# A hybrid convolution and delta-rule block on one core: convolutions without zero margins, large tiles of 4,096 bytes from an address that is a multiple of 256, and a new order of the first half

## The chip, the core and the metric

The kernel runs on one core of a Trainium2 chip, in one launch. The metric is device time in microseconds, the median of three runs. The core has five engines with a queue each: TensorE (PE, matrix products into eight PSUM banks), VectorE (DVE), ScalarE (ACT), GpSimd (POOL) and SyncE (SP). In this kernel SP issues all transfers between the on-chip SBUF and HBM. "PEld" in the profile is TensorE's weight load, which runs beside its products.

## What is computed

One layer on 1,024 positions with 1,024 channels, all in float32. The part that the change touches, from the reference:

```python
h = rms_norm(x, g_mix[i])
proj = h @ w_in[i]
glu_a, glu_b, q, k, v, z, a_in, b_in, gate_a, gate_b = split_cols(proj, IN_SIZES)

c = glu_a * jax.nn.sigmoid(glu_b)
c = depthwise_conv(c, conv_dw_w[i]) + conv_dw_b[i]
c = jax.nn.silu(layer_norm(c, conv_ln_g[i], conv_ln_b[i]))
y_conv = c @ w_conv_out[i]

qkv = jax.nn.silu(depthwise_conv(jnp.concatenate([q, k, v], axis=-1), qkv_conv_w[i]))
```

The first convolution is 31 positions wide, the second 5. Both are centred and run per channel over the positions, with zeros outside. Behind them come the gated delta rule on q, k and v (eight heads, forward and backward), an output product for each branch, a merge by two gates, a product with `w_o`, a gated feed-forward part of width 2,816 and a per-layer embedding with a gate.

## The kernel before

**Layout and products.** Channels lie on the 128 partitions and positions along the free dimension, so a block is 128 channels by 1,024 positions, worked on in two halves of 512. A float32 operand of a large product is split into two parts of type float32r, high and low (`split`, line 709: ScalarE makes the high part, VectorE the rest), and each product is three matmuls (`mm3`, line 760): high by high, high by low, low by high. The stationary operand is mostly a weight tile w (128 x 128 of it at a time), the moving one 512 columns of a large tile. Matmuls of 128 columns in plain float32 serve the delta rule and the transposes.

**Two halves.** The first half is the input projection (eight blocks each of q, k, v, z, of the two halves of the GLU and of two gates), the two convolutions, the layer norm with the first output product, and the delta rule of the heads. The second half is the output product of the delta rule, the merge, `w_o`, the feed-forward part and the embedding.

**Who sets the order.** The program first records its operations (`Plan.add`, line 191), each with an engine, a cost and a level. `Plan.order` (line 347) then runs through them as through a simulation: on each engine it picks, of what is ready, the operation of the lowest level, and it hands out the slots of the tiles as they come free. The levels of the parts stand in `LV` (line 573), the number of tiles that a part may hold in `CAP` (line 574): `raw5` and `acc5` are the input and the result of the short convolution, `wmain` and `wfill` the weight tiles of the main stream and of the fill, `bank` the PSUM banks of small products. `MAIN` (line 607) and `FILL` (line 609) list the blocks of the projection in the order in which they are recorded: `k0` is block 0 of k, `g0` the GLU with its wide convolution, `a4` and `b5` blocks of the two gates, `l0` the decay and beta logits, `p0` the projection of the embedding. Every block of the projection loads its weights in two transfers of 256 KB (`load_w`, line 718), and most store their result.

**Where tiles lie.** SBUF is given out in this order: constants, 32 large slots (line 633), middle tiles of 2,048 bytes (19 of them: 8 + 4 + 4 + 3), small tiles (6,272 bytes), six weight tiles of 4,096 bytes (line 636). A large slot is as wide as the widest tile that ever lies in one. That is c of the wide convolution, [128, 1,024 + 30] floats (line 1027), 4,216 bytes, rounded up to 4,224. The constants end at byte 24,384, so large slots start at 64 and 192 modulo 256 in turn. Weight tiles start at 204,736 and every 4,096 from there, 192 modulo 256. Most high and low parts of a moving operand are the two halves of one slot (`half_pair`, line 776); those of the normed input hT, which the whole projection uses, lie in two slots (`act_pair`, line 773).

**The convolutions.** `do_qkv` (line 979) has ScalarE copy the product from PSUM into a tile with two zero columns at either end, which GpSimd fills, and `conv` (line 963) takes the first tap on ScalarE and four on VectorE, each over 1,024 columns shifted by one. `conv31` (line 997) works on even and odd positions apart: with u the sum of the even part of the input over the sums of neighbouring taps and v, going on from u, a sum over differences of odd and even parts, 31 taps take 46 steps of 512 columns where two separate sums would take 62. Its input c has zero margins that GpSimd fills in three places (lines 1032 to 1034).

Of the kernel before, what the change touches and what calls it, by code (L numbers as in the profile page):

```python
# [15 lines left out]
AF = mybir.ActivationFunctionType  # L16
ALU = mybir.AluOpType
# [527 lines left out]
P = 128  # L545
D = 1024
T = 1024
KB = D // P
NJ = T // P
NH = 8  # L550
CK = 31
SK = 5
# [3 lines left out]
HW = 512  # L556
# [6 lines left out]
def hs(h):  # L563
    return slice(h * HW, (h + 1) * HW)


def cs(j):
# [2 lines left out]


N_BIG, N_MID, N_W, N_D = 32, 8, 6, 11
LV = dict(w=-3.3, logits=-0.2, delta=-1.8, qkv=1.3, glu=1.5, z=-0.4, conv31=2.4, gate=2.3, pl=-0.3, ln=0.3, cout=2.55, ssq=-1.8)
CAP = dict(raw5=6, acc5=3, cpad=10, acc31=1, dif=1, lnev=3, wmain=4, wfill=2, bank=2, x0=4)
LEAD = (1, 3, 4)
PAIRS = (3, 3, 2, 2)
NS = sum(PAIRS)
# [26 lines left out]

MAIN = ("k0 v0 q0 l0 g0 z0 q1 z2 k1 g1 v1 g2 a4 z1 v2 q3 k2 k5 v3 b5 z3 q2 k3 k4 z4 q4 g3 v5 z6 v4 g4 q5 "
        "k7 q6 g6 g5 a7 z5 a5 v6 q7 a6 v7 k6 a0 g7 z7")
FILL = "a2 a3 b7 a1 b2 b0 b1 b3 p0 b4 b6"
PL_AFTER = 2  # L610


def ORDER(f):
# [3 lines left out]
          "a": lambda i: f["do_gate"](0, i), "b": lambda i: f["do_gate"](1, i)}  # L617
    for w in (MAIN + " " + FILL).split():
        do[w[0]](int(w[1:]))
# [5 lines left out]
def hybrid_block(tc, x, p, g_mix, w_in, conv_dw_w, conv_dw_b,  # L625
# [3 lines left out]
    pn = Plan(tc)  # L629
# [12 lines left out]
    def large(shape=None, dtype=F32, line="t", cap=99):  # L642
        return big.tile(shape or [P, T], dtype, tag="big", line=line, cap=cap)
# [9 lines left out]

    proj_cap, bank_cap = [2], [CAP["bank"]]

    def ev2():
        return medium()
# [8 lines left out]
    def const(name, shape):  # L666
        return cp.tile(shape, tag=name)
# [11 lines left out]
    for _ in range(WARM):  # L679
        ps = ps_.tile([P, HW], tag="ps", line="warm", cap=1)  # L680
# [7 lines left out]
    ident2 = const("ident2", [64, 32])  # L688
    pn.tt(ident2, ident[:64, 0:32], ident[:64, 32:64], ALU.add)

    half16 = const("half16", [P, 16])
    pn.fill(half16, 0.5)
    mhalf16 = const("mhalf16", [P, 16])
    pn.fill(mhalf16, -0.5)

    beta = const("beta", [P, 16, NJ])
# [7 lines left out]
    pl_s = const("pl_s", [P, 2, NJ])  # L704
    taps = const("taps", [P, KB, CK + 3 * SK])
    cw31s = const("cw31s", [P, KB, CK // 2 + 1])


    def split(hi, lo, src, scale=None):
# [8 lines left out]
    def load_w(w, r0, nk, c0, cap=4, pool=None):  # L718

        lv, parts = pn.level, []  # L720
        st = "main" if pn.stream == "main" else "rest"
        pn.level = LV["w"] if 1 <= lv < 3 else lv
        for k0 in range(0, nk, 4):
            n = min(4, nk - k0)
            raw = mid.tile([P, 4, P], tag="raw", bufs=4, line="raw", cap=2 if cap < N_W else 4, stream=st)
            if pool is None:
                t = wp.tile([P, 2, 4, P], F32R, tag="w", line="w", cap=cap, stream=st)
            else:
                t = pool([P, 2, 4, P], F32R, line="hp")
            rows_ = w[(r0 + k0) * P:(r0 + k0 + n) * P, c0:c0 + P]  # L730
            pn.dma(raw[:, :n], rows_.rearrange("(k q) c -> q k c", q=P))
            split(t[:, 0, :n], t[:, 1, :n], raw[:, :n])
            parts.append(t)
        pn.level = lv
        return parts
# [20 lines left out]
    def gated(out, t, v):  # L756

        pn.stt(out, t, 1.0, v, ALU.add, ALU.mult)
# [58 lines left out]
    x0 = [large(line="xt", cap=8) for _ in range(8)]  # L817
# [8 lines left out]
    col = {}  # L826
    def vectors(r, names):
        r0, vr = r, medium([64, P], line="vr")
        for name, v in names:
            n = v.shape[1] // P  # L830
            pn.dma(vr[r - r0:r - r0 + n, :], v[0].rearrange("(k q) -> k q", q=P))
            col[name] = vec_t[:, r:r + n]
            r += n
        ps = bank()
        pn.transpose(ps[:, :r - r0], vr[:r - r0], ident[:r - r0, :r - r0])
        pn.copy(vec_t[:, r0:r], ps[:, :r - r0])
        return r


    n = vectors(0, VEC[:1])  # L840
    pn.stream = "main"
    first = MAIN.split()[0]
    first_w = [load_w(w_in[0], 0, KB, C_Q + ("qkv".index(first[0]) * NH + int(first[1:])) * P)]
# [19 lines left out]
    def x_turned(h, k):  # L863
        ps = ps_.tile([P, HW], tag="ps", line="x0", cap=CAP["x0"])
        for i in range(4):
# [17 lines left out]
    NT = CK + 3 * SK  # L883
    raw = large([NT, D], line="taps")
# [4 lines left out]
    ps = bank()  # L889
# [6 lines left out]

    pn.tt(cw31s[:, :, :CK // 2], taps.at(0, [(NT, KB), (2, CK // 2)]), taps.at(1, [(NT, KB), (2, CK // 2)]), ALU.add)
    pn.copy(cw31s[:, :, CK // 2:], cw31[:, :, CK - 1:])


    to(0.4, "start")
# [7 lines left out]
    def logits():  # L909
        to(LV["logits"], "logits")  # L910
        wr = medium([P, KB, 32], line="wab")
# [47 lines left out]

    def load_cols(c0, cap=CAP["wmain"]):  # L960
        return load_w(w_in[0], 0, KB, c0, cap)

    def conv(acc, src, w, n, bias=None):
        pn.act(acc, src[:, 0:T], AF.Copy if bias is None else AF.Identity, scale=w[:, 0:1], bias=bias)
        for t in range(1, n):
            pn.stt(acc, src[:, t:t + T], w[:, t:t + 1], acc, ALU.mult, ALU.add)

    d_qkv = [[dp.tile([P, T], tag="dqkv%d_%d" % (i, j), bufs=1) for j in range(NH)] for i in range(3)]
    d_kk = [dp.tile([P, T], tag="dkk%d" % j, bufs=1) for j in range(NH)]
    d_y = [[spill() for _ in range(2)] for _ in range(KB)]  # L970
# [8 lines left out]
    def do_qkv(which, hd):  # L979
        to(LV["qkv"], "main", "qkv")  # L980
        b = which * NH + hd
        w = first_w.pop() if first_w else load_cols(C_Q + b * P)
        raw = large([P, T + SK - 1], line="raw5", cap=CAP["raw5"])
        for h in range(2):
            ps = block_half(w, hA, h, KB)
            pn.act(raw[:, 2 + h * HW:2 + (h + 1) * HW], ps)
        pn.fill(raw[:, 0:2], 0.0)
        pn.fill(raw[:, T + 2:T + 4], 0.0)
        acc = large(line="acc5", cap=CAP["acc5"])
        conv(acc, raw, taps[:, hd, CK + which * SK:CK + (which + 1) * SK], SK)  # L990
        pn.act(acc, acc, AF.Silu)
        pn.dma(d_qkv[which][hd], acc)

    lnacc = large(line="lnacc")
    CH = (T + CK - 1) // 2

    def conv31(c, b):

        w, ws = cw31[:, b], cw31s[:, b]
        co, ce = c[:, :CH], c[:, CH:2 * CH]
        dif = large([P, 2, CH], line="dif", cap=CAP["dif"])
        pn.tt(dif[:, 0], ce, co, ALU.subtract)
        pn.tt(dif[:, 1, :CH - 1], ce[:, 1:], co[:, :CH - 1], ALU.subtract)
        acc = large([P, 2, HW], line="acc31", cap=CAP["acc31"])
        u, v = acc[:, 0], acc[:, 1]
        pn.act(u, co[:, 0:HW], AF.Identity, scale=ws[:, 0:1], bias=col["cb31"][:, b:b + 1])
        n = CK // 2
        for t in range(1, n + 1):  # L1010
            pn.stt(u, co[:, t:t + HW], ws[:, t:t + 1], u, ALU.mult, ALU.add)
        for t in range(n + 1):
            pn.stt(c.at(0, [(2, HW)]) if t == n else v, dif[:, 0, t:t + HW], w[:, 2 * t:2 * t + 1],
                   v if t else u, ALU.mult, ALU.add)
        for t in range(n):
            pn.stt(c.at(1, [(2, HW)]) if t == n - 1 else u, dif[:, 1, t:t + HW], w[:, 2 * t + 1:2 * t + 2],
                   u, ALU.mult, ALU.add)

    def do_glu(b):
        to(LV["glu"], "main", "glu")  # L1020
        wb = load_cols(C_GLUB + b * P)
        sg = [ev2(), ev2()]
        for h in range(2):
            half_tanh(sg[h], block_half(wb, hA, h, KB))
        wa = load_cols(C_GLUA + b * P)

        c = large([P, T + CK - 1], line="cpad", cap=CAP["cpad"])
        for h in range(2):
            pa = block_half(wa, hA, h, KB)
            gated(c.at(7 + h * HW // 2, [(CH + 1, 2), (1, HW // 2)]), sg[h].at(0, [(1, 2), (2, HW // 2)]),  # L1030
                  pa.at(0, [(1, 2), (2, HW // 2)]))
        pn.fill(c[:, 0:7], 0.0)
        pn.fill(c[:, CH - 8:CH + 8], 0.0)
        pn.fill(c[:, 2 * CH - 7:2 * CH], 0.0)
        to(LV["conv31"], "conv31")
        conv31(c, b)
        acc = c[:, :T]
        for h in range(2):
            pn.dma(d_y[b][h], acc[:, hs(h)])
        if b == 0:  # L1040
            pn.copy(lnacc, acc)
        else:
            pn.tt(lnacc, lnacc, acc, ALU.add)

    def do_gate(i, b):
        to(LV["gate"], "fill", "gate")
        w = load_cols((C_GA, C_GB)[i] + b * P, CAP["wfill"])
# [468 lines left out]
    for k in range(HK):  # L1516
        raw = [large([P, 2, HW], line="o", cap=O_CAP) for _ in range(2)]
# [48 lines left out]
    for b in range(0, KB, 2):  # L1566
# [6 lines left out]
        s = medium(line="gs", cap=1)  # L1573
# [5 lines left out]
        g1 = mid.tile([P, HW], tag="m2", line="p1", bufs=4)  # L1579
# [56 lines left out]
    for h in range(2):  # L1636
        pn.sec = "wo"

        n = WO_LEAD if h == 0 else 0
# [15 lines left out]
        for k in range(HK):  # L1655
            for b in (k, k + HK):
                v = xT[b][:, hs(h)]
# [143 lines left out]
    ws = []  # L1801
# [132 lines left out]
    p0 = 0  # L1934
# [68 lines left out]
    for t in range(NJ - 1):  # L2003
# [3 lines left out]
        for c in range(2):  # L2007
            v = x3[t][:, hs(c)]
# [4 lines left out]
    t, n = NJ - 1, HW // 2  # L2013
    e = x3[t]
    v = [e[:, HW + i * n:HW + (i + 1) * n] for i in range(2)]
# [46 lines left out]
```

## Time and profile before

| | |
|---|---|
| median of three runs | 2059.19 us (2057.17 to 2059.95) |
| span of the profiled execution | 2056.1 us |
| TensorE busy | 2032.3 us (99%), 9,985 matmuls |
| VectorE busy | 1591.0 us (77%) |
| ScalarE busy | 1109.6 us (54%) |
| GpSimd busy | 123.8 us (6%) |
| transfers | 288.6 MB, 43.3% of the time of 16 DMA engines |

The span is that of one profiled execution, from its first to its last instruction; the runs are timed from outside, 3.1 us above it. "Busy" counts a matmul from its start to its modelled end, and the next one starts before that, so the time that a matmul takes in a stream is read from the distance of starts. Stretches of time are given in us from the span's start.

### The profile page before, as it was taken

To read this page: it belongs to the slowest core of one execution; us is meant where nothing else is said; L and a number is where in the kernel's file an instruction comes from. 1 tells how busy PE (TensorE), PEld (TensorE's weight loads), DVE (VectorE), ACT (ScalarE), POOL (GpSimd) and SP (SyncE) were. 2 spreads that over 40 slices of the span, in tenths; PEclk is the share of its full clock that TensorE was granted. 3 is DMA by queue.
4 is the path that set the end of the run, shared out by engine and by line. 5 is a ranking of instruction groups with operands and counts; after the bars stand their busy time and mean duration, and the time that the engine had idled before them with its cause. 6 is when DMAs were issued, how large, how long until landed. Compare 5 with 4: busy or idle time off the path is not lost.

```text
span 2056.1 us, 29043 instructions
## 1 busy us (share of the span) xinstructions
PE 2032.3 (99%) x9985; PEld 1670.9 (81%) x9985; DVE 1591.0 (77%) x2814; ACT 1109.6 (54%) x2627; POOL 123.8 (6%) x211
## 2 busy tenths in 40 slices
PE   8999999999999999999999999999999999999998
PEld 6888788888888888888888788887878877887887
DVE  5549999877959999997587876796666657889955
ACT  7635674566766675747865554433333335434462
POOL 1000111001100210011100000000000000000010
PEclk9999999999999999999999999999999999999999
DMA  5532432443333332534578676433323328534232
GB/s 195 167 97 98 140 108 89 149 136 103 112 127 127 108 95 85 200 113 165 175 256 277 199 251 190 144 114 106 103 89 116 102 82 292 169 110 130 86 107 103
DMA packets 278753, 288.60 MB, mean 140 GB/s; under 512 B 17767, under 2 KB 196128, under 8 KB 278606
## 3 DMA queue, kind: packets, MB, share of 16 engines
q1 hardware_dynamic: 278606, 286.76, 43.3%
q8 instruction: 78, 1.28, 0.3%
q14 instruction: 69, 0.57, 0.1%
HBM read 201.16 MB, written 85.53 MB: 139 GB/s over the span
## 4 chain that ended last, share of the span: by engine, by line
PE 73%; DVE 5%; ACT 4%; issue 1%; DMA 1%; POOL 0%; SPq 0%; POOLq 0%; DVEq 0%; ACTq 0%
PE ps L244 72%; DVE big L292 4%; ACT big L269 2%; PE ps L249 1%; ACT big L276 1%; DMA big<-d 1%; ACT w L269 1%; DVE mid L292 1%; DVE w L292 0%; ACT m L276 0%; DMA big<-dg 0%; ACT ps L276 0%; POOL rn L321 0%; DVE xin L292 0%; ACT mid L269 0%
## 5 line engine op out<-in xcount | busy, mean ns | idle before, releaser
L244 PE MATMUL ps<-big,w 128*128 128x512 f32 x6972 | 1707.3, 398 | 2.9 <-ACT big L269 1.6
L244 PEld LDWEIGHTS ps<-big,w 128*128 128x128 f32 x6972 | 1284.5, 188 | 290.6 <-ACT mid L269 4.8
L269 ACT CAST w<-raw 128x512 fp32r<-128x512 f32 (+2 forms) x298 | 176.5, 596 | 285.5 <-PE ps L244 237.0
L292 DVE SCALAR_TENSOR_TENSOR big<-big,taps 128x512 f32<-128x512 f32 (+1 forms) x344 | 299.6, 905 | 11.8 <-ACT big L276 8.1
L292 DVE TENSOR_TENSOR w<-raw,w 128x512 fp32r<-128x512 f32 (+2 forms) x298 | 198.3, 669 | 97.7 <-ACT w L269 95.9
L269 ACT CAST w<-mid 128x512 fp32r<-128x512 f32 (+2 forms) x205 | 113.5, 558 | 148.0 <-PE ps L244 109.2
L292 DVE TENSOR_TENSOR big<-big 128x512 fp32r<-128x512 f32 (+4 forms) x259 | 177.0, 710 | 8.3 <-ACT big L269 3.7
L292 DVE TENSOR_TENSOR w<-mid,w 128x512 fp32r<-128x512 f32 (+2 forms) x205 | 124.7, 612 | 52.0 <-ACT w L269 51.7
L292 DVE TENSOR_TENSOR big<-ps,big 128x512 f32<-128x512 f32 (+1 forms) x172 | 117.8, 691 | 28.4 <-PE ps L244 20.9
L269 ACT COPY big<-ps 128x512 f32<-128x512 f32 (+3 forms) x194 | 84.0, 445 | 61.2 <-PE ps L244 44.5
L269 ACT COPY big<-big 32x128 f32<-32x128 f32 (+1 forms) x264 | 104.9, 443 | 22.2 <-DVE big L292 18.3
L244 PEld LDWEIGHTS ps<-big 128*128 128x128 f32 x706 | 98.1, 190 | 19.2 <-issue 7.6
L269 ACT CAST big<-big 128x512 fp32r<-128x512 f32 x162 | 95.0, 621 | 34.1 <-DVE big L292 29.8
L244 PE MATMUL ps<-big 128*128 128x128 f32 (+2 forms) x706 | 108.7, 298 | 3.8 <-ACT big L269 2.0
L292 DVE SCALAR_TENSOR_TENSOR big<-big,cw31s 128x512 f32<-128x512 f32 x120 | 92.9, 774 | 6.3 <-ACT big L276 4.1
L244 PE MATMUL ps<-w,big 128*128 128x512 f32 (+1 forms) x294 | 81.2, 403 | 0.2 <-DVE w L292 0.2
L244 PEld LDWEIGHTS ps<-S,big 128*128 128x128 f32 x448 | 68.5, 190 | 10.9 <-DVE S L292 3.8
L244 PE MATMUL ps<-S,big 128*128 128x128 f32 x448 | 76.8, 277 | 0.4 <-DVE S L292 0.4
L269 ACT COPY mid<-ps 128x512 f32<-128x512 f32 x72 | 42.2, 592 | 60.9 <-PE ps L244 57.7
L244 PEld LDWEIGHTS ps<-big,m 128*128 128x128 f32 x512 | 61.3, 191 | 10.1 <-ACT m L276 8.8
L276 ACT ACTIVATE big<-big 128x1024 f32<-128x1024 f32 (+2 forms) x80 | 56.9, 717 | 21.6 <-DVE big L292 17.5
L244 PE MATMUL ps<-big,m 128*128 128x128 f32 x512 | 66.2, 279 | 1.1 <-ACT m L276 1.0
(185 smaller groups left out, 1773.7 us busy)
## 6 DMA issues: line engine op xcount, KB each, us to landing
raw<-in_w_in_dram SPq DMA_DIRECT2D x128, 256.0 KB, 3.0
mid<-d SPq DMA_DIRECT2D x128, 256.0 KB, 3.6
d<-big SPq DMA_DIRECT2D x122, 256.0 KB, 3.2
big<-d SPq DMA_DIRECT2D x118, 256.0 KB, 5.3
d<-mid SPq DMA_DIRECT2D x99, 256.0 KB, 2.1
big<-dqkv SPq DMA_DIRECT2D x32, 512.0 KB, 4.1
raw<-in_w_gate_up_dram SPq DMA_DIRECT2D x49, 256.0 KB, 3.1
dqkv<-big SPq DMA_DIRECT2D x24, 512.0 KB, 2.9
```

What stands on the lines that cost most here:

```text
L244: o = self.add("pe", lambda: self.nc.tensor.matmul(out.ap(), lhsT.ap(), rhs.ap(), start=start, stop=stop, **kw), [out], [lhsT, rhs], cost)
L249: self.add("pe", lambda: self.nc.tensor.transpose(out.ap(), in_.ap(), ident.ap()), [out], [in_, ident], 0.11)
L269: return self.nc.scalar.copy(out.ap(), in_.ap())
L276: return self.nc.scalar.activation(out.ap(), in_.ap(), func, **kw)
L292: return getattr(e, name)(**{k: v.ap() if isinstance(v, View) else v for k, v in kw.items()})
```

## The change

It rewrites both convolutions so that no tile has margins: a tap with shift s is added only onto the columns that have a neighbour at that distance (`taps_onto`, new), starting from the middle tap, which covers all columns. In the wide convolution v is now a sum of its own, started by ScalarE, and one addition joins u and v. One short step of eight columns, with the taps in reversed order (`cw31r`, a new constant of 8 x 8 floats), adds what the last column gives beyond the end. So the widest large tile is [128, 1,024] floats, 4,096 bytes. Two constants of 16 columns are cut to the 8 that are used. With the new constant the constants now end at byte 24,576, a multiple of 256. Middle and small tiles and weight tiles keep their sizes and their order behind the large ones. `LV`, `CAP`, `MAIN` and `FILL` are drawn up anew.

```diff
-LV = dict(w=-3.3, logits=-0.2, delta=-1.8, qkv=1.3, glu=1.5, z=-0.4, conv31=2.4, gate=2.3, pl=-0.3, ln=0.3, cout=2.55, ssq=-1.8)
-CAP = dict(raw5=6, acc5=3, cpad=10, acc31=1, dif=1, lnev=3, wmain=4, wfill=2, bank=2, x0=4)
+LV = dict(w=-2.4, logits=0.0, delta=-1.7, qkv=1.3, glu=1.5, z=-0.6, conv31=2.2, gate=2.3, pl=-0.6, ln=0.4, cout=2.35, ssq=-1.9)
+CAP = dict(raw5=4, acc5=4, cpad=10, acc31=1, dif=1, lnev=3, wmain=5, wfill=4, bank=4, x0=4)
...
-MAIN = ("k0 v0 q0 l0 g0 z0 q1 z2 k1 g1 v1 g2 a4 z1 v2 q3 k2 k5 v3 b5 z3 q2 k3 k4 z4 q4 g3 v5 z6 v4 g4 q5 "
-        "k7 q6 g6 g5 a7 z5 a5 v6 q7 a6 v7 k6 a0 g7 z7")
-FILL = "a2 a3 b7 a1 b2 b0 b1 b3 p0 b4 b6"
+MAIN = ("k0 v0 q0 l0 b5 z0 q1 g0 z2 k1 g1 v1 g2 z1 q3 v3 a4 q4 k5 k2 z3 q2 k3 k4 z4 g3 v2 v5 v4 g4 k7 q5 "
+        "q6 g6 g5 z5 a0 a5 v6 b0 q7 a6 v7 k6 g7 a7 z7")
+FILL = "a1 z6 b3 b2 a2 b4 b7 a3 b1 p0 b6"
...
-    half16 = const("half16", [P, 16])
+    half16 = const("half16", [P, NJ])
...
-    mhalf16 = const("mhalf16", [P, 16])
+    mhalf16 = const("mhalf16", [P, NJ])
...
+    cw31r = const("cw31r", [P, KB, CK // 4 + 1])
...
+    pn.copy(cw31r, taps.at(CK - 1, [(NT, KB), (-2, CK // 4 + 1)]))
...
-    def conv(acc, src, w, n, bias=None):
-        pn.act(acc, src[:, 0:T], AF.Copy if bias is None else AF.Identity, scale=w[:, 0:1], bias=bias)
-        for t in range(1, n):
-            pn.stt(acc, src[:, t:t + T], w[:, t:t + 1], acc, ALU.mult, ALU.add)
+    def taps_onto(acc, src, n, tap, shifts):
+
+        for s in shifts:
+            a, b = max(0, -s), n - max(0, s)
+            pn.stt(acc[:, a:b], src[:, a + s:b + s], tap(s), acc[:, a:b], ALU.mult, ALU.add)
+
+    def conv(acc, src, w):
+        m = SK // 2
+        pn.act(acc, src, AF.Copy, scale=w[:, m:m + 1])
+        taps_onto(acc, src, T, lambda s: w[:, m + s:m + s + 1], [s for s in range(-m, m + 1) if s])
...
-        raw = large([P, T + SK - 1], line="raw5", cap=CAP["raw5"])
+        raw = large(line="raw5", cap=CAP["raw5"])
...
-            pn.act(raw[:, 2 + h * HW:2 + (h + 1) * HW], ps)
-        pn.fill(raw[:, 0:2], 0.0)
-        pn.fill(raw[:, T + 2:T + 4], 0.0)
+            pn.act(raw[:, hs(h)], ps)
...
+        ev, od = c[:, :HW], c[:, HW:]
+        dif = large([P, 2, HW], line="dif", cap=CAP["dif"])
+        pn.ts(dif[:, 0, 0:1], ev[:, 0:1], -1.0, ALU.mult)
+        pn.tt(dif[:, 0, 1:], od[:, :HW - 1], ev[:, 1:], ALU.subtract)
+        pn.tt(dif[:, 1], od, ev, ALU.subtract)
...
+        others = [s for s in range(-MID, MID + 2) if s]
+        pn.act(u, ev, AF.Identity, scale=ws[:, MID:MID + 1], bias=col["cb31"][:, b:b + 1])
+        taps_onto(u, ev, HW, lambda s: ws[:, s + MID:s + MID + 1], others)
+        pn.act(v, dif[:, 0], AF.Copy, scale=w[:, 2 * MID:2 * MID + 1])
+        taps_onto(v, dif[:, 0], HW, lambda s: w[:, 2 * (s + MID):2 * (s + MID) + 1], others)
+        n = MID + 1
+        pn.stt(v[:, HW - n:], cw31r[:, b], od[:, HW - 1:], v[:, HW - n:], ALU.mult, ALU.add)
+        pn.tt(c.at(0, [(2, HW)]), v, u, ALU.add)
+        taps_onto(u, dif[:, 1], HW, lambda s: w[:, 2 * (s + MID) + 1:2 * (s + MID) + 2], others[:-1])
+        pn.stt(c.at(1, [(2, HW)]), dif[:, 1], w[:, 2 * MID + 1:2 * MID + 2], u, ALU.mult, ALU.add)
...
-        c = large([P, T + CK - 1], line="cpad", cap=CAP["cpad"])
+        c = large(line="cpad", cap=CAP["cpad"])
...
-        pn.fill(c[:, 0:7], 0.0)
-        pn.fill(c[:, CH - 8:CH + 8], 0.0)
-        pn.fill(c[:, 2 * CH - 7:2 * CH], 0.0)
```

More of the change, by code (lines that the diff above doesn't have):

```diff
@@ L982, in do_qkv @@
         w = first_w.pop() if first_w else load_cols(C_Q + b * P)
-        raw = large([P, T + SK - 1], line="raw5", cap=CAP["raw5"])
+        raw = large(line="raw5", cap=CAP["raw5"])
         for h in range(2):
             ps = block_half(w, hA, h, KB)
-            pn.act(raw[:, 2 + h * HW:2 + (h + 1) * HW], ps)
-        pn.fill(raw[:, 0:2], 0.0)
-        pn.fill(raw[:, T + 2:T + 4], 0.0)
+            pn.act(raw[:, hs(h)], ps)
         acc = large(line="acc5", cap=CAP["acc5"])
-        conv(acc, raw, taps[:, hd, CK + which * SK:CK + (which + 1) * SK], SK)
+        conv(acc, raw, taps[:, hd, CK + which * SK:CK + (which + 1) * SK])
         pn.act(acc, acc, AF.Silu)
@@ L994, in hybrid_block @@
     lnacc = large(line="lnacc")
-    CH = (T + CK - 1) // 2
+    MID = CK // 4
     def conv31(c, b):
         w, ws = cw31[:, b], cw31s[:, b]
[L1002 to L1005, printed above, removed]
+        ev, od = c[:, :HW], c[:, HW:]
[3 more added lines that the diff above has]
+        pn.tt(dif[:, 1], od, ev, ALU.subtract)
         acc = large([P, 2, HW], line="acc31", cap=CAP["acc31"])
         u, v = acc[:, 0], acc[:, 1]
[L1008 to L1017, printed above, removed]
+        others = [s for s in range(-MID, MID + 2) if s]
[8 more added lines that the diff above has]
+        pn.stt(c.at(1, [(2, HW)]), dif[:, 1], w[:, 2 * MID + 1:2 * MID + 2], u, ALU.mult, ALU.add)
     def do_glu(b):
@@ L1025, in do_glu @@
         wa = load_cols(C_GLUA + b * P)
-        c = large([P, T + CK - 1], line="cpad", cap=CAP["cpad"])
+        c = large(line="cpad", cap=CAP["cpad"])
         for h in range(2):
             pa = block_half(wa, hA, h, KB)
-            gated(c.at(7 + h * HW // 2, [(CH + 1, 2), (1, HW // 2)]), sg[h].at(0, [(1, 2), (2, HW // 2)]),
+            gated(c.at(h * HW // 2, [(HW, 2), (1, HW // 2)]), sg[h].at(0, [(1, 2), (2, HW // 2)]),
                   pa.at(0, [(1, 2), (2, HW // 2)]))
-        pn.fill(c[:, 0:7], 0.0)
-        pn.fill(c[:, CH - 8:CH + 8], 0.0)
-        pn.fill(c[:, 2 * CH - 7:2 * CH], 0.0)
         to(LV["conv31"], "conv31")
         conv31(c, b)
-        acc = c[:, :T]
         for h in range(2):
-            pn.dma(d_y[b][h], acc[:, hs(h)])
+            pn.dma(d_y[b][h], c[:, hs(h)])
         if b == 0:
-            pn.copy(lnacc, acc)
+            pn.copy(lnacc, c)
         else:
-            pn.tt(lnacc, lnacc, acc, ALU.add)
+            pn.tt(lnacc, lnacc, c, ALU.add)
     def do_gate(i, b):
```

## The prediction

> **What bounds the kernel now.** I read the busy times of the page first, then the stretches of time, then the groups by line and tile of TensorE, and last single stretches of its timeline. The page, and busy time by stretch (stretch in us, then its length, PE, PEld, DVE, ACT, POOL busy with counts, granted clock, DMA share, GB/s):
>
> ```profile
> span 2056.1 us, 29043 instructions
> PE 2032.3 (99%) x9985; PEld 1670.9 (81%) x9985; DVE 1591.0 (77%) x2814; ACT 1109.6 (54%) x2627; POOL 123.8 (6%) x211
> ...
> 0.00:50.00 50.00, 44.30 (x228) 34.18 (x229) 28.90 (x55) 36.74 (x70) 5.79 (x20) 0.97 0.59 190
> 100.00:200.00 100.00, 100.00 (x461) 81.84 (x460) 65.93 (x122) 45.16 (x106) 1.90 (x6) 1.00 0.33 108
> 200.00:300.00 100.00, 97.73 (x553) 82.57 (x551) 94.39 (x163) 64.52 (x175) 15.94 (x26) 1.00 0.34 105
> 700.00:800.00 100.00, 99.33 (x606) 85.71 (x605) 97.24 (x169) 64.42 (x184) 15.42 (x26) 1.00 0.33 105
> 900.00:1000.00 100.00, 97.40 (x589) 82.56 (x587) 65.96 (x122) 82.02 (x240) 14.51 (x21) 1.00 0.50 166
> 1500.00:1600.00 100.00, 100.00 (x433) 80.10 (x432) 62.91 (x95) 36.47 (x62) 0.00 (x0) 1.00 0.33 105
> 2000.00:2056.00 56.00, 48.72 (x234) 40.35 (x232) 32.19 (x58) 15.16 (x34) 4.32 (x8) 0.98 0.29 99
> ```
>
> TensorE is idle for 2056.1 - 2032.3 = 23.8 us in all. Of these 5.7 lie in the first 50 us and 7.3 in the last 56, so 10.8 are left for everything between. The second half, from some 1034 us on, has next to none. So neither VectorE nor the DMA sets the end, and there are two ways to move it by more than a few microseconds: the time that one matmul takes, or new idle time. The granted clock is 1.00, so the clock leaves nothing to win. The groups of TensorE by line, with shapes kept apart, and the matmuls that use a weight tile w, by half of the kernel:
>
> ```profile
> L244 PE MATMUL ps<-big,w 128*128 128x512 f32 x6972 | 1707.3, 398 | 2.9 <-ACT big L269 1.6 <-ACT m L269 0.7 <-ACT w L269 0.2
> L244 PE MATMUL ps<-w,big 128*128 128x512 f32 x282 | 79.5, 408 | 0.2 <-DVE w L292 0.2
> ...
> 0.00:1034.00 1034.00, 823.92 (x3137) 568.38 (x3138) 93.24 (x133) 81.81 (x134) 1.00 0.40 129
> 1034.00:2056.00 1022.00, 963.44 (x4130) 768.44 (x4129) 229.16 (x370) 208.00 (x370) 1.00 0.48 152
> ```
>
> Some 7,260 matmuls of 512 columns between a large tile and a weight tile fill most of the span (3,137 + 4,130 by the second view). The duration of one, 398 ns, overlaps the next; what counts is the distance from start to start. In the timeline a row of n matmuls in a stream gives it as (length - the last one's duration)/(n - 1). The median duration is 392 ns by the first row here (minimum/median/maximum); the other four rows are long streams of both halves (start, length, operation, tiles, count):
>
> ```profile
> L244 PE MATMUL ps<-big,w x432: 387/392/468, 1399.8 to 1499.9; 128*128 128x512 f32 x144
> ...
> 100.52 59.67 PE L244 MATMUL ps<-big,w 128*128 128x512 f32 x257
> 352.21 44.44 PE L244 MATMUL ps<-big,w 128*128 128x512 f32 x192
> 1307.13 91.17 PE L244 MATMUL ps<-big,w 128*128 128x512 f32 x394
> 1748.68 55.61 PE L244 MATMUL ps<-big,w 128*128 128x512 f32 x240
> ```
>
> That makes 231.6 and 230.6 ns in the first half (mean 231.1), and 231.0 and 231.0 in the second. A change of 1 ns here is worth 7.3 us of the end. This is the number on which the change has to act, and the only one large enough.
>
> **Where the rate comes from.** The change moves addresses, so I ask what the rate has to do with them. The allocation of the kernel before puts large slots at 64 and 192 modulo 256 in turn (24,384 + 4,224 i) and every weight tile at 192. I took from the kernel's own allocation in which slots the tiles of a stream lie, and chose streams of one kind. First two whose moving tiles all lie at 192, like the weights (odd slots 27, 19, 1, 23, 13, 3 and 3, 19, 17, 9, 27, 25, 21); then three whose moving tiles all lie at 64, so 128 bytes off the weights modulo 256 (even slots 24, 14, 12, 6, 10, 8; then 22, 8, 28, 20, 18, 24; then 2, 14, 16, 12, 6, 10):
>
> ```profile
> 1309.75 4.25 PE L244 MATMUL ps<-big,w 128*128 128x512 f32 x18
> 1101.36 4.95 PE L244 MATMUL ps<-big,w 128*128 128x512 f32 x21
> ...
> 1365.71 4.33 PE L244 MATMUL ps<-big,w 128*128 128x512 f32 x18
> 1047.58 4.36 PE L244 MATMUL ps<-big,w 128*128 128x512 f32 x18
> 1819.99 4.33 PE L244 MATMUL ps<-big,w 128*128 128x512 f32 x18
> ```
>
> Like the weights: (4.25 - 0.392)/17 = 226.9 and (4.95 - 0.392)/20 = 227.9 ns. 128 off: 231.6, 233.4 and 231.6 ns, mean 232.2. Is it the place of the moving tile, or its place against the weights? In the last stage the roles change: the moving tile is w, always at 192, and the stationary one is a large tile, at 64 in the first row here and at 192 in the second:
>
> ```profile
> 1971.38 2.25 PE L244 MATMUL ps<-w,big 128*128 128x512 f32 x9
> 1983.12 2.21 PE L244 MATMUL ps<-w,big 128*128 128x512 f32 x9
> ```
>
> With the same last duration, (2.25 - 0.392)/8 = 232.3 against (2.21 - 0.392)/8 = 227.3 ns. The moving side is alike in both, so it is the difference of the two addresses that matters: equal modulo 256 some 227, 128 apart some 232. (The weights of the next matmul are loaded while this one streams: PEld is busy 81% beside PE's 99%, so both reads run at once.) The 231 of the long streams is the mixture.
>
> **The change part by part.** *Addresses.* The two constants of 16 columns go to 8, 64 bytes less in all; the reversed taps add 8 x 8 x 4 = 256 bytes. The first large tile so moves from 24,384 to 24,576, which is 0 modulo 256, and with slots of 4,096 bytes all large tiles lie at 0. The weights come after 32 x 4,096 bytes of large tiles, 19 x 2,048 of middle ones and 6,272 of small ones, of which the change touches no size but the first: 200,832, which is 128 modulo 256. So each large tile lies 128 off each weight tile: the mixture goes, and it goes to the slow kind. At 232.2 ns the sum is 3,137 x 1.1 + 4,130 x 1.2 ns = 3.5 + 5.0 = +8.5 us. The ends by the quoted rows: at 231.6, 1.6 + 2.5 = +4 us; at 233.4, 7.2 + 9.9 = +17 us. I take +8, nearer the two rows that agree. What the trace can't show is a start at 0 modulo 128, since all tiles stood at 64 modulo 128 before; if that alone did the fast kind, the sum has the other sign (first rival).
>
> *The convolutions.* Rows of the taps on VectorE, of the first tap and bias on ScalarE, of the smallest VectorE copy, of a plain two-operand step, and of the margins' fills:
>
> ```profile
> L292 DVE SCALAR_TENSOR_TENSOR big<-big,taps 128x512 f32<-128x512 f32 x248 | 175.6, 752 | 1.4
> L292 DVE SCALAR_TENSOR_TENSOR big<-big,taps 128x1024 f32<-128x1024 f32 x96 | 124.6, 1298 | 10.4 <-ACT big L276 8.1
> L292 DVE TENSOR_TENSOR big<-ps,big 128x512 f32<-128x512 f32 x168 | 115.1, 691 | 27.3 <-PE ps L244 20.9 <-ACT big L276 5.8
> L292 DVE COPY cw31s<-taps 128x8 f32<-128x8 f32 x1 | 0.2, 169 | 0.0
> L276 ACT ACTIVATE big<-big,vec_t,cw31s 128x512 f32<-128x512 f32 x8 | 6.5, 816 | 0.0
> L325 POOL MEMSET big<- 128x2 f32 x48 | 3.5, 98 | 112.7 <-PE ps L244 80.9 <-DMA dqkv<-big 11.4 <-DVE big L292 7.7
> L325 POOL MEMSET big<- 128x7 f32 x16 | 1.6, 103 | 7.4 <-ACT big L269 7.4
> L325 POOL MEMSET big<- 128x16 f32 x8 | 0.9, 111 | 101.8 <-DVE big L292 101.8
> ```
>
> Per GLU block the wide convolution had 46 steps of 512 columns on VectorE. Now it has 44 steps that are up to 8 columns shorter, one step of full width that writes the last result, one plain addition (0.691 for 0.752 us), and two tiny ones (a column, and eight columns; about 0.2 us each by the copy of eight): +0.34 us. The shorter steps save 184 columns, at (1298 - 752)/512 = 1.07 ns each 0.2 us. Over eight blocks that is +1 us of VectorE's 1591. The 24 short convolutions keep their four steps, six columns shorter: -0.15 us in all. ScalarE gets one more first tap per block, 8 x 0.816 = 6.5 us, in stretches where it is busy 45 to 82 of 100 us. GpSimd loses the 72 fills, 6.0 us of an engine 6% busy. All of this is hidden behind matmuls as long as VectorE keeps up. Where it is fullest, 97.24 of 100 us between 700 and 800, the cover is thin; even fully exposed, the net of VectorE is 1 us. I put it at 0, bounds -1 to +1.
>
> *The order.* Five weight tiles may be taken ahead for the main stream and four for the fill (4 and 2 before), four banks instead of two, four raw tiles instead of six; one gate block (b5) goes ahead of z0, GLU 0 behind q1, and so on. Each moved block takes its two weight loads of 256 KB and its stores with it through SP's queue, past the loads of the blocks it overtakes. The count of blocks, loads and matmuls is as before. What there is to win is TensorE's idle time in the first half, which is what its waits add up to, longest first:
>
> ```profile
> PE ps L244 <- ACT big L269: 3.7, 5, 1.5
> PE ps L244 <- DVE xin L292: 2.4, 3, 1.2
> ```
>
> None is longer than 1.5 us at a time, and the stretches above show 2.3 us (200 to 300), 0.7 (700 to 800) and 2.6 (900 to 1000). All idle time between the ends is 10.8 us; a better order wins at most some 9 of these, and I let a worse one lose as much (fewer raw tiles make the matmuls of q, k and v wait for VectorE sooner just where it is 94 to 97% busy). Both are open, and nothing in the profile favours either: 0, from -9 to +9. Sum: 2056.1 + 8.5 + 0 + 0 = 2064.6 us of span. The runs shown stand 2059.19 - 2056.1 = 3.1 us above that span, which I keep: **2067.5 us**.
>
> **The rivals.** *First, faster:* the alternation between the two kinds of slots, or the start at 64 modulo 128, is what costs, and uniform tiles at a multiple of 256 stream at the fast rate whatever the weights' place. At 227.4 ns, the mean of the two fast rows, 3,137 x 3.7 + 4,130 x 3.6 ns = 26.5 us go: 2033 us. For it: the fast streams are uniform. Against it: the three slow streams are uniform too, and so are the two of the last stage, which differ in the stationary tile alone. It decides from the first stream at all: if the rate is under 229 ns the sign turns. *Second, no change:* a stream's rate doesn't hang on the weights' address, and the difference of the rows is of another cause, such as the stage they stand in; then 231 ns stays and the time is 2059, with the order's part about it. For it: the second rate of the slow kind (231.6) is close to the mixture. Against it: the two rows 12 us apart in the same stage. The Trainium skill, in "TensorE: Matmul & The Clock Gate", section "Part 2: What happens when you issue a matmul", says this: TensorE reads moving data and weights through two independent ports, and loading the next weights takes nothing from the running matmul. By that rule the addresses change nothing; the trace's 232.3 against 227.3 speaks against it. *Third, the order alone:* the waits of the first half go while the rate stays, 2059 - 9 = 2050 us; the waits' shortness is for it, VectorE's 94 to 97% against it.
>
> **How the numbers follow.** Less than 0.2%, 4 us, can't be told from no change here. Forecast 0.5, from 2059.19 + 4 to 2059.19 + 17 us and the order's part about that; first rival 0.2; second 0.2; third 0.1. Most of the forecast's own range lies above 2063: slower 0.43 and same 0.07. The second gives same 0.12 and 0.04 on each side, the third faster 0.08 and same 0.02, the first faster 0.2. In sum faster 0.32, same 0.21, slower 0.47. The range reaches at the top to 2078 (the slow row's +17 and 2), and at the bottom to 2044, which takes in the second and third rivals and what half of the first would give (2059 - 13 = 2046), and leaves out its full size.
>
> **What would show it.** In the profile after, long streams of matmuls of big and w start some 232 ns apart in both halves, with no streams near 227; in the last stage the same. Count them in a stretch: 433 in 100 us of the gate and up products now, then 430. VectorE's sum stays within 5 us of 1591, ScalarE's rises by some 6, GpSimd's falls by some 6. TensorE's idle time stays between 15 and 33 us. Wrong would be streams at 227 to 229 ns, streams unchanged at 231, or idle time of over 33 us in the first half.

## The result, and the profile after

The changed kernel takes 2066.51 us (2066.11 to 2068.14), the kernel before, run again beside it, 2058.31: a ratio of 1.0043 (95% interval 1.0031 to 1.0055), so slower by 0.43%. The prediction was 2067.5 us, slower with a chance of 0.47.

The page of the changed kernel, its stretches (columns as before the change: length, PE, PEld, DVE, ACT, POOL busy with counts, granted clock, DMA share, GB/s), its weight matmuls between 1400 and 1500 us (minimum/median/maximum duration) and a long stream of the timeline (start, length, operation, tiles, count):

```profile
span 2064.9 us, 28958 instructions
...
PE 2041.4 (99%) x9985; PEld 1671.7 (81%) x9985; DVE 1591.6 (77%) x2831; ACT 1113.6 (54%) x2633; POOL 120.9 (6%) x139
```

```profile
0.00:50.00 50.00, 44.70 (x230) 34.79 (x231) 29.65 (x56) 37.38 (x71) 5.40 (x14) 0.97 0.59 199
...
200.00:300.00 100.00, 98.20 (x553) 81.97 (x552) 95.50 (x168) 65.33 (x177) 15.25 (x17) 1.00 0.31 98
700.00:800.00 100.00, 98.31 (x595) 83.82 (x594) 95.10 (x162) 67.73 (x189) 13.22 (x17) 1.00 0.31 106
900.00:1000.00 100.00, 97.26 (x609) 83.26 (x607) 70.67 (x137) 77.25 (x225) 12.90 (x18) 1.00 0.46 151
...
1500.00:1600.00 100.00, 100.00 (x428) 79.42 (x427) 60.35 (x92) 35.54 (x61) 0.00 (x0) 1.00 0.33 105
```

```profile
L244 PE MATMUL ps<-big,w x429: 387/393/479, 1399.7 to 1499.8; 128*128 128x512 f32 x143
```

```profile
1312.75 107.47 PE L244 MATMUL ps<-big,w 128*128 128x512 f32 x461
```

The span grew by 8.8 us. TensorE's busy time grew by 9.1 and its idle time went from 23.8 to 23.5, so the same 9,985 matmuls take longer, and TensorE waits no longer in sum. VectorE's sum moved by 0.6 us. In the stretch from 1500 to 1600, where TensorE never stops, 428 matmuls fit where 433 did. The stream gives (107.47 - 0.393)/460 = 232.8 ns from start to start, against 231.0 before.

The addresses are those that the prediction worked out: of the matmuls of 512 float32r columns, all 7,254 between a large and a weight tile have them 128 bytes apart modulo 256. I also took the distance of starts over all neighbours in the trace (leaving out steps of 245 ns and more, which hold a wait or a switch to another kind of matmul): 231.2 ns before, 232.5 after. At 1.37 ns for some 7,070 steps this is 9.7 us, the whole difference. One group went the other way. In the last stage six of the sixteen weight tiles of the gate are large tiles, so 126 matmuls have both operands in large tiles, at 0 alike. Two rows of that stage, first with the moving operand in a weight tile, then with both in large tiles:

```profile
2007.80 4.36 PE L244 MATMUL ps<-w,big 128*128 128x512 f32 x18
2018.84 4.26 PE L244 MATMUL ps<-big 128*128 128x512 f32 x18
```

The last matmul's duration taken as 0.393, that is 233.4 against 227.5 ns in one execution, in the same stage and loop: 18 matmuls each, that differ in where the moving tile lies.

### The profile page after: what moved, and what is told of

Read it like the earlier page. It is cut to its first block, busy times and chain, and to the rows that moved or that the text cites. A ratio compares the mean times of both kernels' runs of the same rounds, so it can differ in the third digit from the quotient of the medians.

```text
span 2064.9 us, 28958 instructions
## 1 busy us (share of the span) xinstructions
PE 2041.4 (99%) x9985; PEld 1671.7 (81%) x9985; DVE 1591.6 (77%) x2831; ACT 1113.6 (54%) x2633; POOL 120.9 (6%) x139
## 4 chain that ended last, share of the span: by engine, by line
PE 84%; DVE 7%; ACT 6%; issue 1%; DMA 1%; POOL 0%; SPq 0%; POOLq 0%; DVEq 0%; ACTq 0%
PE ps L244 83%; DVE big L292 6%; ACT big L269 4%; PE ps L249 1%; DVE w L292 1%; ACT big L276 1%; DVE mid L292 1%; ACT w L269 1%; ACT m L276 1%; DMA big<-dg 0%; DMA big<-in_x_dram 0%; POOL xrs L321 0%; ACT L276 0%; DMA mid<-in_conv_ln_g_dram 0%; DMA d<-mid 0%
## 5 line engine op out<-in xcount | busy, mean ns | idle before, releaser
L292 DVE SCALAR_TENSOR_TENSOR big<-big,taps 128x1023 f32<-128x1023 f32 (+8 forms) x336 | 306.3, 913 | 17.2 <-ACT big L276 12.8
L292 DVE TENSOR_TENSOR big<-big 128x512 fp32r<-128x512 f32 (+3 forms) x267 | 180.9, 700 | 7.4 <-ACT big L269 3.7
L292 DVE SCALAR_TENSOR_TENSOR big<-big,cw31s 128x505 f32<-128x505 f32 (+7 forms) x120 | 91.0, 758 | 3.8 <-ACT big L276 3.6
L269 ACT COPY m<-ps 128x512 f32<-128x512 f32 x48 | 28.2, 587 | 77.2 <-PE ps L244 77.2
```

The lines of the kernel that those rows point to most:

```text
L269: return self.nc.scalar.copy(out.ap(), in_.ap())
L292: return getattr(e, name)(**{k: v.ap() if isinstance(v, View) else v for k, v in kw.items()})
```

## The experiments

All experiments compute the whole block. Times are medians; the ratios are to the kernel before, run on the same chip. The two runs that change one cap alone were on another chip than the rest, so they are compared by their ratios.

**Weights moved to the same place as the large tiles.** The theory: the difference of the addresses of the moving and the stationary operand modulo 256 sets the rate of a stream. The two last small tiles are made 64 bytes wider each, which moves the weight tiles, and only them, by 128 bytes. The order of the instructions is the same on each engine.

```diff
-        fr = tin.tile([P, 1], tag="fr", bufs=2)
+        fr = tin.tile([P, 24], tag="fr", bufs=2)[:, 0:1]
...
-    fr = tin.tile([P, 1], tag="fr", bufs=2)
+    fr = tin.tile([P, 24], tag="fr", bufs=2)[:, 0:1]
```

> The kernel after, with the two last small tiles 64 bytes wider each, so that the weight tiles start 128 bytes later and lie at 0 modulo 256 like the large tiles. Nothing else moves. Theory (the difference of the two addresses sets the rate): streams of big and w go from 232.5 ns to 227 to 228, some 7,260 matmuls by 4.5 to 5.5 ns, so 33 to 40 us less than after, 2027 to 2034 us, also below the kernel before. Rival one (the place of the large tile alone counts, or its uniformity): the rate stays at 232.5 and the time at 2066. Rival two (the new order or the conversion of the convolutions made the kernel slower): the time stays within a few us of 2066 as well, since neither is touched.

Measured: 2039.55 us, ratio 0.9916 (0.9900 to 0.9933). Its page, its weight matmuls between 1400 and 1500 us, a long stream, and a row of the last stage:

```profile
span 2036.8 us, 28958 instructions
...
PE 2012.3 (99%) x9985; PEld 1669.3 (82%) x9985; DVE 1587.4 (78%) x2831; ACT 1112.5 (55%) x2633; POOL 123.1 (6%) x139
```

```profile
L244 PE MATMUL ps<-big,w x439: 387/389/484, 1399.8 to 1499.8; 128*128 128x512 f32 x147
```

```profile
1297.94 122.30 PE L244 MATMUL ps<-big,w 128*128 128x512 f32 x537
...
1974.57 4.24 PE L244 MATMUL ps<-w,big 128*128 128x512 f32 x18
```

The stream runs at (122.30 - 0.389)/536 = 227.4 ns, and in the last stage the moving weight tile now at (4.24 - 0.389)/17 = 226.5 ns, where it was at 233.4. TensorE's busy time fell by 29.1 us. Both rivals said that the time would stay at 2066; both fall. The theory's rate came as expected, its time only in part: 27 us less than after instead of 33 to 40. Counting in the trace, the last large matmul starts 28.2 us earlier than after, and the 3,165th (the end of the first half, roughly) 8.3 us earlier, where 3,165 times 5.1 ns would be 16. So the second half gave nearly all that the rate promised (20 us of 4,295 times 5.1 ns, 22 us) and the first half only half of it. By the starts in the trace, only some 2,800 of its steps lead from one large matmul straight to the next; they took 12.0 us less. The steps to, from and among the small matmuls took 3.6 us more. VectorE is 95% busy there in the stretches shown above, but the wait of TensorE that grew most ends at ScalarE (total, times, longest; after, then this version):

```profile
PE ps L244 <- ACT big L269: 3.5, 6, 1.0
...
PE ps L244 <- ACT big L269: 6.2, 5, 1.6
```

TensorE's idle time up to that matmul is 15.1 and 15.6 us, so little of the shortfall is added waiting in sum; what slows the small matmuls stays open. This version also beats the kernel before, by 0.84%.

**All addresses 64 bytes later.** The two constants go back to 16 columns (the diff is that of the change, undone for `half16` and `mhalf16`). Large tiles lie at 64 modulo 256, weights at 192; differences stay.

> The kernel after with the two constants of 16 columns as they were, so that large tiles lie at 64 modulo 256 and weights at 192: every address 64 bytes later, all differences unchanged. Theory: no change, 2066 us and 232.5 ns. Rival (the place modulo 128 or 256 counts by itself): another rate, up or down by 1 ns or more, 7 us or more.

Measured: 2063.97 us, ratio 1.0032 (1.0020 to 1.0044), where after has 1.0043 (1.0031 to 1.0055). A long stream of it:

```profile
1309.83 110.50 PE L244 MATMUL ps<-big,w 128*128 128x512 f32 x474
```

(110.50 - 0.393)/473 = 232.8 ns, as after, and the intervals of the two ratios overlap. So 64 bytes more for every tile show no effect: the place itself, at 0 or 64 modulo 128, doesn't matter, and this was what the prediction could not see in the trace.

**Weights 64 bytes and 160 bytes later than after.** The same widening of the small tiles by other amounts: weights at 192, then at 32, large tiles at 0.

```diff
+        fr = tin.tile([P, 16], tag="fr", bufs=2)[:, 0:1]
...
+        t = tin.tile([n, P + 8], tag="rT", bufs=1)[:, :P]
```

The first line alone (in both places) is the kernel with weights at 192; the one with weights at 32 has the second line and `[P, 24]`.

> The kernel after with the weight tiles 64 bytes later: large tiles at 0, weights at 192 modulo 256, so 64 off. Uniform streams, as in after (128 off, 232.5 ns) and with the weights at 0 (0 off, 227.5 ns). If only equal addresses are fast: 232 ns or more, 2064 us or more. If the rate falls with the distance: some 230 ns, 2050 us. If 64 bytes are as good as equal: 227.5 ns, 2040 us.

> The kernel after with the weight tiles 160 bytes later: large tiles at 0, weights at 32 modulo 256. If only equal addresses are fast: 232 ns or more, 2064 us or more. If the rate falls with the distance: near 228.5 ns, 2044 us. If what counts is whether both lie in the same 64 or 128 bytes: 227.5 ns, 2040 us.

Measured: 2051.04 us (ratio 0.9974, 0.9960 to 0.9987) with weights at 192, and 2068.29 (1.0052, 1.0035 to 1.0069) with weights at 32. A long stream and a row of the last stage with weights at 192, then a stream with weights at 32:

```profile
1304.42 115.89 PE L244 MATMUL ps<-big,w 128*128 128x512 f32 x504
...
1985.73 4.36 PE L244 MATMUL ps<-w,big 128*128 128x512 f32 x18
```

```profile
1312.31 107.90 PE L244 MATMUL ps<-big,w 128*128 128x512 f32 x461
```

With weights at 192 the stream runs at (115.89 - 0.392)/503 = 229.6 ns, near the middle case of the expectation. But the last stage, where the moving tile is the one at 192, runs at 233.4. So 64 one way is not 64 the other way, and distance is not the rule. With weights at 32 it is (107.90 - 0.396)/460 = 233.7 ns (0.392 and 0.396 are the median durations of these two kernels), where a rule by distance would have it near the best; only the case that leaves equal addresses alone as the fast ones fits this run.

**Slots of 4,128 bytes.** One large tile is made 32 bytes wider, so that all slots are, and the differences run through 0, 32 and so on to 224 within one kernel.

```diff
+        c = large([P, T + 8], line="cpad", cap=CAP["cpad"])[:, :T]
```

> The kernel after with one large tile widened by 32 bytes, so that the slots are 4,128 bytes apart and stand 0, 32, 64 and so on to 224 modulo 256 off the weights, in turn. It shows the rate by difference of the addresses. Theory: slow at 128, fast at 0; between them unknown. If it is banks of 128 bytes, rates rise evenly from 0 to 128 and fall again to 256; if only equal addresses are fast, all differences but 0 are slow. Time between 2050 and 2068 us. Rival (uniform tiles matter, not differences): slower than after throughout, 2070 or more, and no pattern by difference.

Measured: 2062.77 us (one execution). Mean distance of starts by the moving tile's address minus that of the weights that load beside it, modulo 256, over all neighbours below 245 ns, from the starts in the trace:

| difference | 0 | 32 | 64 | 96 | 128 | 160 | 192 | 224 |
|---|---|---|---|---|---|---|---|---|
| ns | 232.0 | 232.2 | 231.6 | 233.8 | 232.0 | 232.3 | 231.0 | 233.6 |
| steps | 683 | 902 | 646 | 1196 | 799 | 1044 | 886 | 575 |

The time lies in the range given, but none of the patterns holds: equal addresses are not fast here (232.0 ns), the rates neither rise to 128 nor fall from it, and the time lies below what the rival expected. A matmul whose own two operands agree gains nothing when its neighbours' tiles lie elsewhere. Together with the uniform kernels (227.4 at 0) this points to a rule for the whole stream: moving tiles have to agree among themselves and with the weights. The mixture before the change fits that: there, three matmuls on one moving tile with its weights' remainder took 684.4 ns on average after a tile of the same remainder, and 695.0 after a tile of the other (357 and 281 cases).

**The order by itself.** First the levels, caps and lists of before on the addresses and convolutions of after; then those of after on the kernel before. The diffs are the lines of `LV`, `CAP`, `MAIN` and `FILL` in the change.

> The kernel after with the levels, caps and the two lists of the kernel before: its addresses and convolutions with the old order. Theory: the rate stays at 232.5 ns, the time within 4 us of 2066. Rival (the order made it slower): back to some 2058 with the rate still at 232.5 and TensorE idle some 9 us less.

> The kernel before with the new levels, caps and lists: its convolutions with margins, its slots of 4,224 bytes, and so its mixture of rates. It is the fourth corner beside before, after and the old order on the new convolutions (2091 us). Theory one (levels, caps and lists are fitted to the operations that they order; either pair that doesn't belong together runs out of work for TensorE near the end of the projection): 2070 us or more at a rate of 231 ns, with TensorE idle over 30 us. Theory two (the new lists are simply the better ones, and repaid what the new convolutions cost): 2050 us or less, idle below 20 us.

| | old levels, caps, lists | new ones |
|---|---|---|
| old convolutions, slots of 4,224 | 1 (before) | 1.0021 (1.0011 to 1.0031) |
| new convolutions, slots of 4,096 | 1.0165 (1.0150 to 1.0180) | 1.0043 (1.0031 to 1.0055) (after) |

The medians are 2091.07 us for the old order on the new convolutions and 2061.93 for the new one on the old convolutions. Both expectations for the first missed: it is neither within 4 us of 2066 nor back at 2058, but 25 us slower than after. The page of the first, its stretches about the end of the first half, its longest wait of TensorE (total, times, longest), and the page of the second:

```profile
span 2089.2 us, 28947 instructions
...
PE 2050.4 (98%) x9985; PEld 1682.9 (81%) x9985; DVE 1592.5 (76%) x2831; ACT 1118.2 (54%) x2637; POOL 119.8 (6%) x139
```

```profile
900.00:1000.00 100.00, 86.16 (x461) 70.95 (x459) 75.18 (x137) 62.72 (x177) 14.91 (x18) 0.95 0.41 137
1000.00:1100.00 100.00, 93.56 (x504) 79.26 (x505) 67.20 (x132) 77.35 (x190) 9.77 (x10) 0.93 0.56 185
```

```profile
PE ps L249 <- DVE m L292: 6.4, 3, 5.8
```

```profile
span 2062.1 us, 29043 instructions
...
PE 2036.6 (99%) x9985; PEld 1670.7 (81%) x9985; DVE 1593.1 (77%) x2814; ACT 1111.7 (54%) x2627; POOL 129.1 (6%) x211
```

With the old order TensorE is idle 38.8 us instead of 23.5, 20.3 of them between 900 and 1100 us, and 461 matmuls fit between 900 and 1000 where 609 do after (their kinds differ as well). The granted clock falls to 0.95 and 0.93 in these two stretches, where it is 1.00 after, and TensorE is busy 9.0 us longer in all with the same 9,985 matmuls. With the 15.3 us of idle time that is the whole difference of the spans, 24.3 us. The rate over all its neighbours is that of after (232.4 against 232.5 ns), so this is not the addresses. That too little is left near the end of the projection to fill the waits of the delta rule is how we read these stretches; no run shows it by itself. In the fourth corner the new lists bring nothing to the old convolutions; they cost 0.2%. Theory one had the sign right, but 2061.93 us and 25.5 us of idle time are well short of its 2070 and 30; theory two falls.

**Which part of the order.** The old lists with the new caps; with four banks alone; with the new numbers of weight tiles alone.

```diff
-CAP = dict(raw5=6, acc5=3, cpad=10, acc31=1, dif=1, lnev=3, wmain=4, wfill=2, bank=2, x0=4)
+CAP = dict(raw5=4, acc5=4, cpad=10, acc31=1, dif=1, lnev=3, wmain=5, wfill=4, bank=4, x0=4)
...
+CAP = dict(raw5=6, acc5=3, cpad=10, acc31=1, dif=1, lnev=3, wmain=4, wfill=2, bank=4, x0=4)
...
+CAP = dict(raw5=6, acc5=3, cpad=10, acc31=1, dif=1, lnev=3, wmain=5, wfill=4, bank=2, x0=4)
```

> The kernel after with the old levels and lists but the new caps (weight tiles, banks, raw tiles). It tells what lost the 25 us with the old order. If the caps did it (too few weight tiles and banks for the new convolutions): 2062 to 2072 us, as after. If the order of the blocks did it: 2085 us or more, with the first half over 15 us longer than after.

> The old order on the new convolutions (2091 us) with four banks for small products instead of two, nothing else of the new caps. The new caps all together gave 2072. If the banks are what the delta rule of the last heads lacked: 2068 to 2076 us. If it was the weight tiles: 2086 to 2096.

> The old order on the new convolutions with five and four weight tiles for the main stream and the fill instead of four and two, nothing else of the new caps. If the weight tiles were what was lacking: 2068 to 2076 us. If it was the banks: 2086 to 2096. If both this and the run with four banks come well below 2091, the 2091 is one bad order among many, and any change of a cap leaves it.

Measured: 2072.10 us (ratio 1.0068, 1.0047 to 1.0090) with all new caps, 2084.31 (1.0124, 1.0094 to 1.0153) with four banks, 2079.44 (1.0100, 1.0071 to 1.0129) with the weight tiles. The stretches from 900 to 1100 us of the three, in this order:

```profile
900.00:1000.00 100.00, 93.78 (x557) 78.84 (x555) 68.50 (x130) 79.39 (x228) 16.98 (x22) 0.98 0.46 155
1000.00:1100.00 100.00, 99.50 (x509) 82.97 (x509) 73.02 (x139) 69.03 (x159) 6.52 (x5) 1.00 0.70 222
```

```profile
900.00:1000.00 100.00, 93.41 (x476) 77.02 (x475) 73.48 (x134) 64.21 (x171) 12.79 (x16) 0.95 0.47 156
1000.00:1100.00 100.00, 93.02 (x522) 80.31 (x521) 72.90 (x141) 76.67 (x198) 10.34 (x12) 0.93 0.57 181
```

```profile
900.00:1000.00 100.00, 97.31 (x512) 80.12 (x511) 71.78 (x134) 65.21 (x170) 11.81 (x15) 1.00 0.49 165
1000.00:1100.00 100.00, 89.30 (x512) 76.50 (x510) 74.30 (x145) 74.07 (x198) 11.37 (x13) 0.95 0.56 178
```

The kernel with all new caps lies at the upper edge of what was expected if the caps did it. Of the 1.65% by which the old order on the new convolutions is behind the kernel before, the caps take back 0.97 and the levels and lists a further 0.25, which is within the intervals. Four banks alone take back 0.41 and the weight tiles 0.65, together about as much as all new caps, so neither "the banks" nor "the weight tiles" is the answer, and both expectations of one cause were wrong. It stays open whether 2091 is a loss of the convolutions as such or of one unlucky order: each of the three changes of the caps came out below it, as the last case of the expectation had it, though with four banks only by 0.41%, some 8 us, and with intervals that touch. Which convolution needs which place was not tried.

## Why the prediction was right

**The bound** was right: TensorE was busy 99% before and after, and the whole difference is in its busy time.

**The rate** was right in direction and size, and in its mechanism for the two cases that the change needs: uniform streams (all moving tiles alike modulo 256, and all stationary ones) with equal addresses, and with addresses 128 apart. The step said that each large tile would lie 128 bytes off each weight tile and that the streams would run at 232.2 ns, worth +8.5 us; they run at 232.8 in the long stream and 232.5 on average, and TensorE's busy time grew by 9.1. It was read from pairs of streams of the kernel before, and what made it safe was the last stage, where the roles of the two tiles are swapped. The sum left out the matmuls of that stage whose operands both lie in large tiles, which became faster (227.5 ns); they are 126, and for them the sign "no streams near 227; in the last stage the same" did not come.

As a general rule, "it is the difference of the two addresses that matters" is too simple: 64 bytes one way and the other gave 229.6 and 233.4 ns, and equal addresses in a mixed stream 232.0. So the 231 of the long streams before is not the plain mixture that the prediction took it for. In the trace before, again over neighbours below 245 ns, 3,565 steps with equal remainders took 230.5 ns on average and 3,076 with remainders 128 apart 231.9; a mixture of 227.4 and 232.5 in these shares would be 229.8. The forecast didn't suffer, since it went from the measured 231 to the slow rows.

The sum itself has two small slips, of 0.2 and 1.3 us. 2064.6 + 3.1 is 2067.7 and not 2067.5; and the 3.1 us set a median against the span of another execution, where one execution's own time and span differ by 1.8 (2066.66 and 2064.9 for the profiled one after).

**The second rival**, by which addresses change nothing, fell with the two kernels that differ in nothing but the place of the weights: 2066.51 and 2039.55 us. The page "TensorE: Matmul & The Clock Gate" of the Trainium skill, in "Part 2: What happens when you issue a matmul", has the two reads on independent ports, so that loading weights takes nothing from the running matmul. In this case the place of the weights alone changes the pace: 232.8 ns after, against 227.4 for the same instructions with the weights 128 bytes further on. Whether the load takes bandwidth or something else slows the stream, no run here tells. **The first rival** fell too: uniform tiles at a multiple of 256 run at the slow rate as long as the weights don't agree with them. Its turning point was named rightly: under 229 ns the sign turns, as it did when the weights were moved. **The third rival**, by which the waits go and the rate stays, fell as well: TensorE's idle time is 23.5 us where it was 23.8, and the rate moved.

**The convolutions and the order** were each put at 0, and their sum is near 0, but not for the reasons given. The convolutions' engine work came out as worked out in direction: VectorE +0.6 us (forecast +1, less 0.15), GpSimd -2.9 (forecast -6), ScalarE +4.0 (forecast +6.5). The added pass of ScalarE, and a long tap of the short convolution on VectorE, after the change:

```profile
L276 ACT ACTIVATE big<-big,taps 128x512 f32<-128x512 f32 x8 | 5.8, 722 | 2.0 <-DVE big L292 2.0
...
L292 DVE SCALAR_TENSOR_TENSOR big<-big,taps 128x1022 f32<-128x1022 f32 x48 | 62.0, 1293 | 13.5 <-ACT big L276 12.8
```

What failed is the two bounds, "fully exposed, the net of VectorE is 1 us" for the convolutions and "from -9 to +9" for the order, which was taken from the idle time that was there to win. They treat the two as separate terms, and the four corners show that they are not. With the old order, the new convolutions and addresses cost 1.65%, 34 us, of which the rate explains some 9; the new order then wins 2091.07 - 2066.51 = 25 us back. Taken the other way round, the new order costs the old convolutions 0.21%, and the new convolutions and addresses add 0.22%, less than the rate alone. So neither term has a size of its own; on the first way both are some 25 us and cancel. Against the kernel before, the old order on the new convolutions has 38.8 - 23.8 = 15 us more idle time, and stretches of a lower clock. Our reading is that the new operations change when tiles and banks come free and the planner then orders everything anew; this is argued, not shown. That the forecast was right in the sum of these terms was luck: nothing in the working makes them cancel, and they do only because the lists were redrawn together with the convolutions.

## What to carry to other kernels

When TensorE is full, take the distance of starts in streams of one kind and compare streams whose operands lie differently; here a few ns per matmul were worth more than all the remaining waits, and they could be had by padding a small tile. Aligning one group of tiles did not help by itself and cost 0.43%: the addresses of moving and stationary tiles had to agree modulo 256, throughout a stream. And where a planner sets the order, an edit of a few operations has to be costed together with its order, since bounds from the old idle time don't hold for the new order.

## What the runs showed of the hardware

In this kernel's uniform streams of 512 float32r columns the distance of starts depends on the addresses modulo 256: 227.4 ns when moving tiles and weights agree, 229.6 with the moving tiles at 0 and the weights at 192, 232.8 with the weights at 128, 233.7 with the weights at 32, and 233.4 with the moving tiles at 192 and the stationary ones at 0. In a mixed stream, equal addresses gain little (232.0 ns with slots of 4,128 bytes). Shifting everything alike by 64 bytes changes nothing (232.8). Why these differences matter is not settled by the runs. With the old order on the new convolutions, the granted clock was 0.95 and 0.93 in the two stretches where TensorE idled 20.3 us, and the same matmuls kept TensorE busy 9.0 us longer than after, so the loss was larger than the waits alone.
